# Two of seven low parts of weights moved from VectorE to GpSimd in a two-layer hybrid attention block

## The chip, the cores and the metric

The kernel runs on one core of a Trainium2 chip. The metric is the device time of one execution in microseconds: the median of the runs of a kernel, all made on the same chip. Engines are called by their roles: TensorE (PE, and PEld for its weight loads), VectorE (DVE), ScalarE (ACT), GpSimd (POOL) and SyncE (SP, which issues DMAs).

## What is computed

Two layers of a block that mixes sparse attention with multi-scale pooling, on 528 tokens (16 meta tokens and 512 of x) of width 1024, in float32:

```python
def hybrid_layer(x, norm_g, w_in, ..., w_a, w_b, w_out, cos, sin, k_top):
    h = rms_norm(x, norm_g)
    proj = jnp.einsum('btd,de->bte', h, w_in)
    q, k, v, gate_a, u_b, gate_b, q_idx, k_idx, w_idx, merge = jnp.split(proj, ..., axis=-1)
    ...
    attn = indexer_sparse_attention(q, k, v, q_idx, k_idx, w_idx, k_top).reshape(B, T, D_A)
    y_a = jnp.einsum('bte,ed->btd', attn * jax.nn.silu(gate_a), w_a)
    pooled = multiscale_pool(u_b, pool_w, pool_b, pool_s)
    y_b = jnp.einsum('bte,ed->btd', pooled * jax.nn.silu(gate_b), w_b)
    g_a, g_b = jnp.split(jax.nn.sigmoid(merge), 2, axis=-1)
    return x + jnp.einsum('btd,de->bte', g_a * y_a + g_b * y_b, w_out)
```

The attention of each block of 128 queries keeps the 128 best keys by an index score (top-k) and takes a softmax over them.

## The kernel before

Activations are kept with the width on the partitions and the tokens along the free axis. Each float32 operand of a large product is split into a high part (a cast to a shorter format, made on ScalarE) and a low part (the operand less its high part), and a product is three matmuls: high by high, low activation by high weight, high activation by low weight. PSUM banks are called d (products), a (scores, transposes) and v (attention values).

The projections for gate_a and merge, and half of w_out in the second layer, use a scheme of seven products for a two by two matrix of blocks, in place of eight. `mixed_prep` (line 257) prepares one chunk of weights for that: it names the seven weight operands a11, a12, s2, s1, s3, s4, a22 by the blocks that they are made from. For each, `hi` (line 265) casts the high part on ScalarE and `lo` (line 271) subtracts it for the low part, a 128x512 tile called w in the profile. Three DMAs and subtractions make the sums among them: `first_sum` (line 253) adds the block a11 to a21 by an accumulating DMA of GpSimd's queue (L255 in the profile), line 284 adds s2 to a12 by another one (L284), and VectorE makes s2 (tile s) and s1 (into tile raw). The steps are the items `i0` to `i8`, which are put into a queue. `group_of_products` (line 1044) issues the seven products in the order a11, a12, s2, s1, s3, s4, a22, each of 12 matmuls: for each of four rows of blocks high by high, high by low, and only with the third matmul the low part of the weights. Between the products it takes items from the queue, so that a weight operand is prepared some products ahead. What a product leaves in PSUM goes to ScalarE (`out`, copies p and u) or to VectorE (`total`, the additions c, or sila in a layer's first two groups), and frees the bank.

There are ten such groups in each layer (`mix_gates`, line 1099) and two at the end (`mix_out`, line 1198), 22 in all. In order of time they are numbered 0 to 9 (about 167 to 305 us), 10 to 19 (525 to 660) and 20 and 21 (704 to 726). Beside them runs the attention, a generator from which some steps are taken between products: logits on TensorE; their sum with the selection's mask on VectorE (lt, with the minimum mn, which a 128x2 product then scales); the exponential and the scaling by rs on ScalarE; the first 16 columns, scaled, in pm on GpSimd (L847); and their split px (cast on ScalarE, subtraction on GpSimd, L881).

The order of TensorE's and VectorE's instructions is the written one; that of ScalarE's and GpSimd's is set by the framework's scheduler when the kernel is built. Each engine works in order. The top-k selection on VectorE (MAX and MATCH_REPLACE on tiles sc) has no place of its own. `Metered` wrappers add up an estimated cost of every instruction that is written to TensorE and to VectorE, and after each product `group_done` takes steps of the selection as long as VectorE's estimate lags:

```python
spare[0] += share[0] * (pe.us - seen[0]) - (dve.us - seen[1])
...
while spare[0] > 0 and sel:
```

Of the kernel before, what the change touches and what calls it, by code (L numbers as in the profile page):

```python
# [91 lines left out]
def tile_block(ctx: ExitStack, tc: tile.TileContext, x, meta, w_in, pool_w, w_a, w_b, w_out, rows, hgain, c_tab, out):  # L92
    nc = tc.nc
    act, gp = nc.scalar, nc.gpsimd
    pe, dve = Metered(nc.tensor, pe_cost), Metered(nc.vector, dve_cost)
# [7 lines left out]
    def f(ap):  # L103
        return ap.bitcast(F32)
# [53 lines left out]
    def w_load():  # L158
        if W["load"] < len(chunks):
            c = w_place()  # L160
            for s in range(2):
                w_fetch(c, s)
# [10 lines left out]
    def w_tile():  # L173
        return wpool.tile([128, 1024], F32R, tag="w", name="w", bufs=8)
# [74 lines left out]
    def marked():  # L249

        return tc.issue_after(mark[0]) if mark[0] else nullcontext()

    def first_sum(c):
        if c in mixed:
            gp.dma_start(raws[c][0][:, 1], raws[c][0][:, 0], accum_op=OP.add)  # L255

    def mixed_prep(c):

        r0, r1 = raws[c]
        blk = {"a11": r0[:, 0], "a21": r0[:, 1], "a12": r1[:, 0], "a22": r1[:, 1]}  # L260
        src = {"a11": "a11", "a12": "a12", "a22": "a22", "s3": "a21", "s2": "s2", "s1": "a11", "s4": "a12"}
        ops = ready[c]
        soon = c <= len(chunks) - 2

        def hi(n):
            t = w_tile().rearrange("p (s k e) -> p s k e", s=2, k=4)
            ops[n] = t
            with marked():
                act.copy(t[:, 0], blk[src[n]])  # L269

        def lo(n):
            dve.tensor_sub(ops[n][:, 1], blk[src[n]], f(ops[n][:, 0]))

        def i0():
            hi("a12")
            if soon:
                hi("a11")

        def i1():
            lo("a12")  # L280
            blk["s2"] = tmp.tile([128, 544], F32, tag="L", name="s2", bufs=LB)[:, :512].rearrange(
                "p (k e) -> p k e", k=4)
            dve.tensor_add(blk["s2"], blk["a21"], blk["a22"])
            gp.dma_start(blk["a12"], blk["s2"], accum_op=OP.add)  # L284
            (lo if soon else hi)("a11")

        def i2():
            if not soon:
                lo("a11")
            dve.tensor_sub(blk["a11"], blk["s2"], blk["a11"])  # L290

        def i3():
            hi("s2")

        def i4():
            lo("s2")
            hi("s1")

        def i5():
            lo("s1")  # L300
            hi("s3")

        def i6():
            lo("s3")
            hi("s4")
            first_sum(c + 1)

        def i7():
            lo("s4")
            hi("a22")  # L310

        def i8():
            lo("a22")
            del raws[c]
            w_load()

        def counted(fn):
            def item():
                fn()
                progress[c] += 1  # L320
            return item

        progress[c] = 0
        return [counted(fn) for fn in (i0, i1, i2, i3, i4, i5, i6, i7, i8)]
# [1311 lines left out]
```

## Time and profile before

| | us |
|---|---|
| median of 3 runs | 734.77 (734.75 to 734.92) |
| the profiled execution | 735.03 |
| its span, first to last instruction | 733.2 |
| TensorE busy | 723.7 |
| VectorE busy | 597.2 |
| ScalarE busy | 491.4 |
| GpSimd busy | 262.3 |

TensorE's clock was granted in full over the whole span. A busy time is the union of an engine's instructions. Matmuls overlap, and the ends of their spans are modelled, so that a stall is better read from a matmul's start and the start of the one before it, or from the idle time of the weight loads. Each line of an instruction gives its start, its time, the engine, the line, the operation, the tiles written and read, the shape, the count, and in square brackets the idle time before it with what ended it.

### The profile page before, as it was taken

Reading aid. Unit: us, or ns where it says so; the run is one execution under the profiler, and the core shown is the slowest. Engines: PE = TensorE matmul, PEld = TensorE weight load, DVE = VectorE, ACT = ScalarE, POOL = GpSimd, SP = SyncE. Lnnn points to the kernel's source line nnn. Section 1 sums busy time; section 2 is a strip of 40 time slices with the busy share of each in tenths; the row PEclk is TensorE's granted clock in tenths of the full one; section 3 lists DMA queues with packets and bytes.
Section 4 is the critical chain, followed back from the end, with each engine's and each line's share of the span. In section 5 each row is a group of like instructions: output and inputs, shape, how many; then the busy total and the mean of one; then the engine's idle time right before and its main releaser. Section 6 shows DMA issues by size and latency. Waiting matters only on the chain.

```text
span 733.2 us, 15958 instructions
## 1 busy us (share of the span) xinstructions
PE 723.7 (99%) x5853; PEld 697.0 (95%) x5853; DVE 597.2 (81%) x1488; ACT 491.4 (67%) x1125; POOL 262.3 (36%) x345
## 2 busy tenths in 40 slices
PE   9999999999999999999999999999999999999998
PEld 8999998899999999999999989998899899999997
DVE  6877999998998875894358779999989988768774
ACT  6779635676888886543246796367788888775643
POOL 3751174721223311173256411857042231116210
PEclk9999999999999999999999999999999999999999
DMA  8777755974655333633422788667564554438832
GB/s 268 234 180 166 168 138 116 238 149 91 148 113 136 81 92 97 211 124 130 132 89 87 180 185 200 155 162 163 112 160 105 134 116 91 113 108 269 201 90 71
DMA packets 103566, 106.41 MB, mean 145 GB/s; under 512 B 5008, under 2 KB 83632, under 8 KB 103488
## 3 DMA queue, kind: packets, MB, share of 16 engines
q1 hardware_dynamic: 91888, 74.89, 33.5%
q0 software_dynamic: 11520, 30.41, 23.4%
q8 instruction: 46, 0.75, 0.4%
q14 instruction: 32, 0.26, 0.1%
q10 hardware_dynamic: 80, 0.08, 0.0%
HBM read 66.41 MB, written 8.55 MB: 102 GB/s over the span
## 4 chain that ended last, share of the span: by engine, by line
PE 79%; DVE 12%; issue 4%; ACT 2%; DMA 2%; POOL 1%; DVEq 0%; POOLq 0%; ACTq 0%
PE d L63 65%; PE a L63 10%; PE v L63 4%; DVE w L63 3%; DVE t L63 1%; DVE lt L63 1%; DMA w<-raw 1%; DVE sc L63 1%; DVE m L63 1%; ACT lt L832 1%; DVE zb L63 1%; DVE nf L63 1%; DVE c L63 0%; DMA raw<-s 0%; DVE sila L63 0%
## 5 line engine op out<-in xcount | busy, mean ns | idle before, releaser
L63 PE MATMUL d<-hhi,w 128*128 128x256 f32 (+3 forms) x1392 | 279.2, 292 | 1.6 <-DVE c L63 1.6
L63 PEld LDWEIGHTS d<-hhi,w 128*128 128x128 f32 x1392 | 222.3, 188 | 5.2 <-DVE c L63 2.0
L63 PE MATMUL d<-hlo,w 128*128 128x256 f32 (+3 forms) x696 | 189.8, 289 | 0.0
L63 DVE TENSOR_TENSOR w<-raw,w 128x512 fp32r<-128x512 f32 (+1 forms) x156 | 121.8, 787 | 14.5 <-ACT w L269 14.3
L63 PEld LDWEIGHTS d<-hlo,w 128*128 128x128 f32 x696 | 131.3, 189 | 1.4 <-issue 0.2
L63 PE MATMUL d<-hsum,w 128*128 128x264 f32 (+1 forms) x720 | 95.1, 285 | 0.2
L63 PEld LDWEIGHTS d<-hsum,w 128*128 128x128 f32 x720 | 89.7, 188 | 1.2 <-issue 0.3
L63 PE MATMUL d<-w,hhi 128*128 128x256 f32 x576 | 86.1, 287 | 0.6 <-DVE w L63 0.6
L269 ACT CAST w<-raw 128x512 fp32r<-128x512 f32 x132 | 78.5, 623 | 3.0 <-DMA raw<-s 2.3
L63 PEld LDWEIGHTS d<-w,hhi 128*128 128x128 f32 x576 | 74.7, 188 | 5.3 <-issue 2.9
L255 POOL DMA_DIRECT2D raw<-raw x22 | 20.5, 931 | 109.3 <-DMA raw<-in_w_in_dram 16.3
L63 DVE MATCH_REPLACE8 sc<-m,sc 128x400 f32<-128x400 f32 (+2 forms) x100 | 54.4, 547 | 0.0
L63 DVE MAX8 m<-sc 128x8 f32<-128x400 f32 (+2 forms) x100 | 53.4, 557 | 0.9
L221 POOL DMA_DIRECT2D w<-raw x34 | 31.8, 966 | 60.9 <-ACT w L220 44.7
L832 ACT ACTIVATE lt<-lt,mn,NR 128x144 f32<-128x144 f32 (+3 forms) x64 | 42.2, 661 | 13.2 <-DVE mn L63 13.0
L63 PE MATMUL d<-mhi,w 128*128 128x272 f32 (+2 forms) x192 | 46.1, 326 | 1.0 <-ACT sq L681 0.9
L63 PE MATMUL d<-w,hlo 128*128 128x256 f32 x288 | 45.5, 281 | 0.0
L284 POOL DMA_DIRECT2D raw<-s x22 | 19.2, 871 | 65.5 <-DVE s L63 29.0
L847 POOL TENSOR_SCALAR pm<-lt,rs 128x16 f32<-128x16 f32 x48 | 28.0, 612 | 38.8 <-DVE rs L63 28.6
L753 ACT ACTIVATE r<-a,wab 128x272 f32<-128x272 f32 (+2 forms) x80 | 35.5, 487 | 8.7 <-PE a L63 8.2
L1481 POOL TENSOR_TENSOR hlo<-ta,hhi 128x256 fp32r<-128x256 f32 (+1 forms) x28 | 26.6, 961 | 40.9 <-PE d L63 28.7
L690 POOL TENSOR_TENSOR t<-t,t 128x256 f32<-128x256 f32 (+1 forms) x34 | 30.6, 900 | 24.6 <-DVE t L63 24.3
(259 smaller groups left out, 1566.2 us busy)
## 6 DMA issues: line engine op xcount, KB each, us to landing
raw<-in_w_in_dram SPq DMA_DIRECT2D x88, 256.0 KB, 3.3
w<-raw POOLq DMA_DIRECT2D x34, 512.0 KB, 5.8
raw<-in_w_in_dram SPq DMA_DIRECT2D x32, 512.0 KB, 4.3
raw<-in_w_out_dram SPq DMA_DIRECT2D x12, 512.0 KB, 3.6
raw<-raw POOLq DMA_DIRECT2D x22, 256.0 KB, 4.0
raw<-s POOLq DMA_DIRECT2D x22, 256.0 KB, 3.3
kept<-res SPq DMA_DIRECT2D x16, 264.0 KB, 2.8
res<-kept SPq DMA_DIRECT2D x16, 264.0 KB, 5.2
```

The lines of the kernel that those rows point to most:

```text
L63: return fn(*a, **k)
L221: gp.dma_start(t, raws[c][s], accum_op=OP.add)
L255: gp.dma_start(raws[c][0][:, 1], raws[c][0][:, 0], accum_op=OP.add)
L269: act.copy(t[:, 0], blk[src[n]])
L284: gp.dma_start(blk["a12"], blk["s2"], accum_op=OP.add)
L690: added[0] = gp.tensor_tensor(t1[:m, :256], t1[:m, :256], t2[:m, :256], op=OP.add).ins
L753: act.activation(r[:, n - 1::-1] if i == 0 else r[:, o:o + e], ps[:, :e], AF.Relu, scale=wab[:, i, h:h + 1])
L832: act.activation(L[hh][:, :n], L[hh][:, :n], AF.Exp, scale=NR[:, i, h:h + 1], bias=mn[:, hh:hh + 1], accum_out=sm[:, hh:hh + 1])
L847: (gp if j < 3 else dve).tensor_scalar(pms[i][:, 2 * j + hh, :], L[hh][:, 0:16], rs[:, hh:hh + 1], None, op0=OP.mult)
L1481: pool_end = gp.tensor_sub(hlo[:, j, a:a + n], d, f(hhi[:, j, a:a + n]))
```

## The change

In `lo`, the low parts of the operands s3 and s4 are subtracted by GpSimd (`gp`) and not by VectorE (`dve`); the other five stay. `gp` is not metered, so the selection's rule no longer counts them. The high parts, the DMAs and the products are as before.

```diff
         def lo(n):
-            dve.tensor_sub(ops[n][:, 1], blk[src[n]], f(ops[n][:, 0]))
+            (gp if n in ("s3", "s4") else dve).tensor_sub(ops[n][:, 1], blk[src[n]], f(ops[n][:, 0]))
```

TensorE's instructions stand in the same order as before, row for row. On GpSimd's queue, at the first groups of the first layer, from group 0's sum s2 on (s_2452), the new subtractions (L272) stand between the accumulating DMAs and the pm scalings. Before:

```order
L255 DMA raw<-raw 128x512
L284 DMA raw<-s_2452 128x512
L255 DMA raw<-raw 128x512
L284 DMA raw<-s_2658 128x512
L847 TENSOR_SCALAR pm<-lt,rs 128x16 x4
L255 DMA raw<-raw 128x512
L284 DMA raw<-s_2846 128x512
```

And now:

```order
L284 DMA raw<-s_2452 128x512
L272 TENSOR_TENSOR w<-raw,w 128x512 x2
L255 DMA raw<-raw 128x512
L284 DMA raw<-s_2659 128x512
L847 TENSOR_SCALAR pm<-lt,rs 128x16 x2
L272 TENSOR_TENSOR w<-raw,w 128x512 x2
L847 TENSOR_SCALAR pm<-lt,rs 128x16 x2
L255 DMA raw<-raw 128x512
```

Two subtractions a group went in, behind the group's s2 DMA and in front of the next group's first sum.

On VectorE, at the same groups, a low part (w<-raw,w) goes out and a step of the selection comes in early; the steps are MATCH_REPLACE on sc_993, which before stood 23 rows further on:

```order
 L63 TENSOR_TENSOR mn<-mn,RQ 128x2
-L63 TENSOR_TENSOR w<-raw,w 128x512 x2
+L63 TENSOR_TENSOR w<-raw,w 128x512
+L63 MATCH_REPLACE sc_993<-m_2528,sc_993 128x528
 L63 TENSOR_TENSOR sila<-d,p_2628 128x264
 L63 SCALAR_TENSOR_TENSOR sila<-th,sila 128x264
```

One low part of group 0 left, and the selection's step moved up from group 1.

On VectorE in group 14, in the second layer (s_8176 before, s_8180 now, is that group's s2), where the selection ended before and the steps of the attention for the third block of queries begin (sc_6126):

```order
 L63 SCALAR_TENSOR_TENSOR zb<-th,zb 128x256
-L63 TENSOR_TENSOR w<-raw,w 128x512 x2
-L63 MATCH_REPLACE sc_6126<-m_8094,sc_6126 128x400
-L63 MATCH_REPLACE sc_6178<-m_8116,sc_6178 128x528
-L63 TENSOR_SCALAR sc_6126<-sc_6126 128x400
-L63 TENSOR_SCALAR sc_6178<-sc_6178 128x528
-L63 TENSOR_TENSOR c<-d,p_8254 128x256
+L63 TENSOR_TENSOR w<-raw,w 128x512
+L63 TENSOR_TENSOR c<-d,p_8258 128x256
 L63 RECIPROCAL rs<-sm 128x2
 L63 TENSOR_SCALAR pm<-lt,rs 128x16 x2
-L63 TENSOR_TENSOR w<-raw,w 128x512
```

Both low parts and the end of the selection left this place; the selection now ends in group 13.

## Rows read from the trace of the kernel before

**Rows 1.** The page's head: span, and busy time (share) and instructions by engine

```profile
span 733.2 us, 15958 instructions
PE 723.7 (99%) x5853; PEld 697.0 (95%) x5853; DVE 597.2 (81%) x1488; ACT 491.4 (67%) x1125; POOL 262.3 (36%) x345
```

**Rows 2.** Busy time by stretch: length, PE, PEld, DVE, ACT, POOL, clock, DMA, GB/s

```profile
186.60:223.00 36.40, 36.29 (x304) 35.66 (x304) 36.23 (x97) 29.95 (x76) 10.01 (x14) 1.00 0.59 130
223.00:303.00 80.00, 79.56 (x715) 76.97 (x713) 60.14 (x164) 64.45 (x150) 17.57 (x26) 1.00 0.42 103
...
543.50:587.00 43.50, 41.88 (x352) 40.97 (x351) 43.22 (x117) 37.06 (x96) 13.76 (x18) 1.00 0.56 125
```

**Rows 3.** Timeline of the weight loads: start, time, what, idle time before

```profile
218.54 0.54 PEld L63 LDWEIGHTS d<-hsum,w 128*128 128x128 f32 x4 [0.32 <-DVE w L63]
...
584.81 0.19 PEld L63 LDWEIGHTS d<-hhi,w 128*128 128x128 f32 x1 [1.78 <-DVE c L63]
...
707.29 0.89 PEld L63 LDWEIGHTS d<-osum,w 128*128 128x128 f32 x7 [0.34 <-DVE w L63]
```

**Rows 4.** Timeline of TensorE: the last matmul ahead of that of 584.81

```profile
582.96 0.28 PE L63 MATMUL d<-hhi,w 128*128 128x256 f32 x1
```

**Rows 5.** Timeline in group 14, VectorE and GpSimd

```profile
577.75 0.56 DVE L63 MATCH_REPLACE8 sc<-m,sc 128x400 f32<-128x400 f32 x1
...
579.52 0.42 DVE L63 TENSOR_TENSOR c<-d,p 128x256 f32<-128x256 f32 x1
...
582.37 1.45 DVE L63 TENSOR_TENSOR mn<-mn,RQ 128x2 f32<-128x2 f32 x1
...
582.77 1.02 POOL L881 TENSOR_TENSOR px<-pm,px 128x256 fp32r<-128x256 f32 x1
...
584.35 0.41 DVE L63 TENSOR_TENSOR c<-d,p 128x256 f32<-128x256 f32 x1
```

**Rows 6.** VectorE's groups by shape: count, busy us, mean ns, idle before

```profile
L63 DVE TENSOR_TENSOR w<-raw,w 128x512 fp32r<-128x512 f32 x132 | 90.1, 687 | 14.5 <-ACT w L269 14.3
...
L63 DVE TENSOR_TENSOR ta<-ta,zb 128x256 f32<-128x256 f32 x24 | 14.3, 598 | 0.8
...
L63 DVE TENSOR_TENSOR osum<-ta,osum 128x256 fp32r<-128x256 f32 x16 | 6.0, 420 | 0.6 <-ACT osum L1150 0.5
```

**Rows 7.** Timeline of VectorE and GpSimd around the px of 645 us

```profile
645.58 1.81 POOL L881 TENSOR_TENSOR px<-pm,px 128x256 fp32r<-128x256 f32 x1 [11.18 <-ACT px L880]
...
646.12 0.69 DVE L63 TENSOR_TENSOR w<-raw,w 128x512 fp32r<-128x512 f32 x1
...
646.72 0.42 DVE L63 TENSOR_TENSOR c<-d,u 128x256 f32<-128x256 f32 x1
```

**Rows 8.** Timeline of GpSimd: instructions with two inputs

```profile
113.22 1.09 POOL L1398 TENSOR_TENSOR us<-u 128x543 f32<-128x543 f32 x1 [0.17 <-ACT u L1391]
...
663.17 0.73 POOL L1481 TENSOR_TENSOR hlo<-ta,hhi 128x256 fp32r<-128x256 f32 x1 [14.94 <-PE d L63]
```

**Rows 9.** Timeline in group 13: casts of s3 and s4, product s3

```profile
564.38 1.14 ACT L269 CAST w<-raw 128x512 fp32r<-128x512 f32 x2
...
567.50 1.58 PE L63 MATMUL d<-hsum,w 128*128 128x256 f32 x12
```

**Rows 10.** Timeline of VectorE and GpSimd around the px of 202 us

```profile
202.42 0.74 POOL L881 TENSOR_TENSOR px<-pm,px 128x256 fp32r<-128x256 f32 x1 [0.67 <-ACT px L880]
...
202.47 1.24 DVE L63 TENSOR_TENSOR raw<-s,raw 128x512 f32<-128x512 f32 x1
```

**Rows 11.** Timeline, group 3's start: first low part, third matmul

```profile
200.26 0.69 DVE L63 TENSOR_TENSOR w<-raw,w 128x512 fp32r<-128x512 f32 x1
...
201.33 0.41 PE L63 MATMUL d<-hhi,w 128*128 128x264 f32 x2
```

**Rows 12.** Timeline of VectorE in group 20: the last low part

```profile
711.10 0.69 DVE L63 TENSOR_TENSOR w<-raw,w 128x512 fp32r<-128x512 f32 x1
```

**Rows 13.** Timeline of TensorE, group 20: third matmul of s4

```profile
711.90 0.28 PE L63 MATMUL d<-hhi,w 128*128 128x256 f32 x1
```

## The prediction

> **What bounds the kernel now.** I read the page's head first, then busy time by stretch, then what TensorE's weight loads waited for, then the rows of VectorE and GpSimd at those places. TensorE is busy for 723.7 of 733.2 us, VectorE for 597.2, GpSimd for 262.3 [rows 1]. A change that leaves TensorE's instructions and their order as they are, as this one does, can win only what TensorE now waits, so the reader should look for those waits and not at VectorE's share. The changed work lies in the 22 groups of seven products, 0 to 21 in order of time. Two stretches matter: from 186.6 to 223 us (groups 2 to 4) VectorE is busy 36.23 of 36.40 us, and from 543.5 to 587 us (groups 12 to 14) 43.22 of 43.50; behind the first it has room, 60.14 of 80.00 [rows 2]. In both stretches the top-k selection (MAX and MATCH_REPLACE) runs on VectorE between the low parts. In the groups the weight loads wait for VectorE in a way worth naming at three places: 0.32, 1.78 and 0.34 us [rows 3]. The 1.78 is the prize. Its matmul starts at 584.81, 1.85 us behind the last one at 582.96 [rows 3, 4], where matmuls of this size otherwise follow each other by (1.58 - 0.28)/11 = 0.12 [rows 9]; so 1.73 us are lost. The chain behind it on VectorE: the end of the top-k (577.75 to 579.52), the 128x2 product mn that took 1.45 us, and at 584.35 the addition c that empties the PSUM bank which the next product wants [rows 5]. Beside that long mn GpSimd ran px [rows 5].
>
> **What leaves VectorE.** 44 low parts, two for each of 22 groups. One takes 0.69 us in the mean [rows 6], and what comes behind it starts 0.60 us later (646.12, 646.72) [rows 7]. So 44 x 0.60 = 26.4 us of VectorE's time. Almost none of it is TensorE's: outside the two stretches it falls on idle time.
>
> **What the order does with it.** The two low parts are not metered any more, so the rule that spends VectorE's spare time pulls top-k steps forward. I count in the new order, with 0.60 us for a low part and 0.6 for a top-k step (577.75 to 579.52 holds two replacements and two short closing steps [rows 5]). Up to the s2 sum of group 3 six low parts are gone (3.6 us) and six steps, some 3.5 us, have come forward: VectorE has gained 0.1 us. Up to group 4's it has gained 2.5, since the top-k now ends in group 3 instead of 4, and up to group 5's 6.0. In the second layer it is the same: nothing gained up to group 13, 2.5 us up to group 14, and the top-k is over before the chain of rows 5 begins.
>
> **What GpSimd takes on.** No row has this subtraction on GpSimd. The nearest: two inputs of 256 columns alone, 0.73 us, and of 543 columns, 1.09 [rows 8]. On the line between them 512 columns cost 0.73 + 256 x 0.36/287 = 1.05 us, the lower end. The upper end is the px at 645.58, which took 1.81 us beside VectorE subtractions that also read two SBUF tensors [rows 7]. I take 1.05, since most of the time VectorE is at something else, and keep 1.81. 44 x 1.05 = 46 us fit into GpSimd's 471 idle us. Is it in time? The tightest s3 is group 13's: two casts start at 564.38 and take 1.14 together, so the first is done at about 565.0; the product begins at 567.50 and wants the low part with its third matmul, 0.24 later [rows 9]. That leaves 2.7 us for 1.05 to 1.81, so 0.9 at the least for what stands in front on GpSimd's queue (pm, an accumulating DMA). s4 comes a product later. I cost the wait for GpSimd itself at nothing here; without that cover it would be up to 1 us a group.
>
> The Trainium skill, page "GPSIMD Engine Reference", section "4.1 Engine selection", speaks against the change: elementwise work on a tile belongs on VectorE, since GpSimd is about 2 times slower with two inputs. By that the subtraction would take 2 x 0.69 = 1.4 us, an estimate from that page, and only step 4 of the sum below would grow, by 0.35; the lengths of rows 8 are shorter than that.
>
> **What the two engines cost each other.** At 202.42 GpSimd's px starts, and VectorE's raw subtraction, 0.05 later, takes 1.24 us [rows 10] instead of about 0.69 [rows 6]: it gets through when px is done. At 645.58 it is the other way: px sits through the subtraction of 646.12 and is done 0.67 us after VectorE turned, at 646.72, to the addition c, which reads PSUM [rows 7]. So only instructions with two SBUF inputs wait. The price of one moved subtraction to VectorE lies between 0 (VectorE is in the top-k or reads PSUM) and 1.05 (all of it). The additions ta<-ta,zb, beside which GpSimd subtracts 256 columns, give a middle: 598 ns against 420 for the same size in osum [rows 6], 0.18 more, or 0.26 at 1.05/0.73 the length. I take 0.4 where two meet, between that and the 0.55 of rows 10, and not every one meets: behind s1's low part, when GpSimd starts, the new order mostly has top-k steps.
>
> **The sum.** (1) The wait at 584.81: two low parts of group 14 (1.2 us) and the end of the top-k (577.75 to 579.52, 1.8 us) leave its chain, 3.0 us against 1.73: gone, -1.73. (2) The 0.32 of group 4 goes with its top-k: -0.3. (3) Group 3's first low part is done at 200.95 and wanted at 201.33 [rows 11], 0.38 us to spare; VectorE has gained nothing there and meets group 2's two subtractions, 2 x 0.4: 0.8 - 0.4 = +0.4, and as much by halves in the second layer: +0.3. (4) Group 20: its last low part on VectorE, at 711.10, would start 0.6 earlier, at 710.5; the work before it reads two SBUF tensors without a gap, so s4's subtraction gets through at about 711.1; 711.1 + 1.05 = 712.15 [rows 12], and the third matmul wants it at 711.90 [rows 13]: +0.25. Together -1.73 - 0.3 + 0.4 + 0.3 + 0.25 = -1.1 us. The profiled execution, 735.03 us, would come to 733.9, the median, 734.77, to 733.7. The 1.8 us around the span stay.
>
> **The rivals.** A, everything covered: no meeting costs anything, and 1.73 + 0.32 + 0.34 = 2.4 us go: 732.4. For it: the top-k reads one tensor. Against: the long mn and raw. B, the port, slower: in each full stretch four subtractions (groups 2 and 3, 12 and 13) fall where the order gives VectorE nothing, and each holds it for 0.7 us, two thirds of 1.05. That is 2.8 us late in each, less 0.38 to spare as in rows 11: 2 x 2.4 - 2.0 = +2.8, 737.6. It decides from 0.35 us per subtraction on (8 x 0.35 - 0.76 = 2.0, what steps 1 and 2 win). For it: rows 5 and 10. Against: rows 7, where VectorE kept its pace. The Trainium skill, page "SBUF — State Buffer", section "🔬 SBUF: two separate sides", has it that whoever starts first keeps the shared port pair for the whole instruction and the other fully blocks, which is this rival taken to the letter; rows 10 agree. C, the wait only moves: the chain of rows 5 gets shorter, but the bank is emptied late for another reason (ScalarE's copies, or px), and nothing is left: 734.8. That GpSimd isn't used is excluded by its new order.
>
> **How the numbers follow.** Forecast 42%, centre 733.7, by its terms 732.9 to 734.7; A 15%; B 28%, 735.7 to 738; C 15%. A measurement of this kernel tells about 0.2% (1.5 us) from no change, so faster is under 733.3, slower over 736.2. A third of the forecast and all of A are faster: 0.30. B but for a fifth is slower: 0.22. The rest, 0.48, is within. The range from 732.0 to 737.6 leaves out A's lowest part and B's upper half.
>
> **What the next profile would show.** Step 1: no wait near 583 us, and MATCH_REPLACE over before group 14. Step 3: a weight load that waits for VectorE's w near 201. Step 4: one that waits for GpSimd near 712. For the price: the 128x512 subtraction on GpSimd at 1.05 to 1.5 us in the mean. If mn, raw and zb on VectorE are longer by over 0.35 us per moved subtraction, B is right. If weight loads wait for GpSimd's w in many groups, my 2.7 us were wrong.

## The result

The changed kernel takes 738.96 us (median of 6 runs, 737.95 to 739.31) against 734.76 (734.41 to 735.58) for the kernel before on the same chip: 1.0051 times as long, 95% interval 1.0040 to 1.0061. In a second comparison it was 1.0039 (1.0025 to 1.0053). The forecast was a gain of 1.1 us; the kernel lost 4.2.

The page's head of the changed kernel, which answers [rows 1]:

```profile
span 736.2 us, 16046 instructions
PE 724.2 (98%) x5853; PEld 696.8 (95%) x5853; DVE 585.1 (79%) x1444; ACT 492.1 (67%) x1125; POOL 319.5 (43%) x389
```

TensorE's work is the same (723.7 before). VectorE lost 44 instructions but only 12.1 of the 26.4 us forecast, and GpSimd gained 57.2 us, not 46. The busy time of the stretches of [rows 2], in that view's columns, says that TensorE now idles where it was full:

```profile
186.60:223.00 36.40, 35.83 (x300) 35.07 (x299) 33.48 (x85) 29.72 (x77) 18.07 (x21) 1.00 0.58 129
223.00:303.00 80.00, 78.75 (x708) 76.16 (x708) 55.29 (x151) 64.00 (x151) 30.53 (x35) 1.00 0.43 100
543.50:587.00 43.50, 41.05 (x342) 39.68 (x342) 40.21 (x103) 36.30 (x96) 19.54 (x23) 1.00 0.55 122
```

TensorE issues the same matmuls in the same order, so the two traces can be laid over each other: the start of a group's first matmul less its start before, and how that grows over a group. Over groups 0 to 21 it grows by 3.11 us, and in the second profile of the same kernel by 3.08, no place differing by more than 0.05. Ahead of group 0, where the change has done nothing yet, those two executions differ by 1.09 us (first matmul at 167.02 and 168.11): so much moves from one execution to the next. The two intervals, 2.9 to 4.5 us and 1.8 to 3.9 us, both hold the 3.1 us, and those are taken for the change here. By place, with the experiments told below beside it ("counted" is e1_metered, "order" e2_order_only, "pm away" e4_pm_away, "halves" e6_halves, "both" e9_halves_counted):

| us | changed | counted | order | pm away | halves | both |
|---|---|---|---|---|---|---|
| group 1 | +0.61 | 0.00 | +0.49 | +0.57 | +0.47 | 0.00 |
| group 2 | +1.13 | +0.64 | +1.77 | +1.49 | +0.13 | 0.00 |
| group 4 | -0.57 | -0.01 | -0.57 | -0.57 | -0.57 | +0.11 |
| group 7 | +0.81 | +0.82 | +0.01 | +0.81 | +0.01 | -0.02 |
| groups 8 to 10 | -0.64 | -0.67 | +0.02 | -0.67 | -0.63 | -0.63 |
| group 12 | +2.15 | +1.10 | +1.55 | 0.00 | +1.29 | +0.01 |
| group 13 | +0.60 | -0.14 | -0.12 | -0.12 | +0.04 | -0.12 |
| group 14, up to a22 | +0.49 | +0.74 | -0.16 | +0.29 | +0.50 | +0.72 |
| group 14, a22 | -1.74 | -1.74 | -1.74 | -1.74 | -1.74 | -1.74 |
| groups 20, 21 | +0.29 | +0.26 | -0.05 | +0.30 | +0.26 | +0.27 |
| all 22 groups | +3.11 | +1.12 | +1.21 | +1.11 | -0.04 | -1.05 |

(The places left out change by at most 0.12, but for three: "pm away" loses 0.65 behind group 14, "halves" 0.19 in group 11, and "both" 0.47 in group 3.) A group is counted to the start of the next one, so that the row "groups 8 to 10" holds the time between groups 9 and 10 as well. The two waits that the prediction meant to win were won, -1.74 and -0.57. What TensorE's weight loads wait for now (start, time, what, in brackets the idle time and what ended it), in groups 1, 2, 7, 12, 12 and 13:

```profile
181.86 0.66 PEld L63 LDWEIGHTS d<-hsum,w 128*128 128x128 f32 x5 [0.46 <-ACT p L1071]
197.90 0.67 PEld L63 LDWEIGHTS d<-hsum,w 128*128 128x128 f32 x5 [0.79 <-ACT u L1071]
273.17 0.78 PEld L63 LDWEIGHTS d<-hsum,w 128*128 128x128 f32 x6 [1.12 <-ACT u L1071]
558.41 0.19 PEld L63 LDWEIGHTS d<-hhi,w 128*128 128x128 f32 x1 [1.51 <-ACT p L1071]
561.28 0.19 PEld L63 LDWEIGHTS d<-hhi,w 128*128 128x128 f32 x1 [0.51 <-DVE c L63]
570.19 0.42 PEld L63 LDWEIGHTS d<-hsum,w 128*128 128x128 f32 x3 [0.55 <-DVE w L63]
```

None waits for GpSimd's w. Mostly it is ScalarE's copy out of PSUM (p, u) that comes late, and VectorE is behind that. The longest, in group 12, from the timelines of GpSimd, VectorE and ScalarE (the row of 1.19 us is the first of the two pm by itself, that of 2.43 both):

```profile
552.75 2.54 POOL L272 TENSOR_TENSOR w<-raw,w 128x512 fp32r<-128x512 f32 x2 [2.45 <-ACT w L269]
...
552.89 1.19 DVE L63 TENSOR_SCALAR pm<-lt,rs 128x16 f32<-128x16 f32 x1
...
552.89 2.43 DVE L63 TENSOR_SCALAR pm<-lt,rs 128x16 f32<-128x16 f32 x2
...
556.95 0.40 DVE L63 TENSOR_TENSOR c<-d,p 128x256 f32<-128x256 f32 x1
...
557.38 0.42 ACT L1117 ACTIVATE c<-c 128x256 f32<-128x256 f32 x1 [2.40 <-DVE c L63]
...
558.00 0.36 ACT L1071 COPY p<-d 128x256 f32<-128x256 f32 x1
```

GpSimd subtracts twice, 552.75 to 555.29. VectorE's two scalings pm, 128 by 16 elements and 0.23 us each elsewhere, take 2.43 together; the first is done at 554.08, 0.04 behind GpSimd's first subtraction (552.75 and 1.29), the second at 555.32, 0.03 behind its second. They sit out one subtraction each. Behind them three selection steps stand ahead of c (556.95), and ScalarE, which works in order, waits 2.40 us for c with the copy p behind it. For p waits the product of 558.41. A blocked instruction shows as a long one here, not as idle time: the reader must compare it with others of its form.

### The profile page after: what moved, and what is told of

The parts are those of the page before. It is cut to its first block, busy times and chain, and to the rows that moved or that the text cites. A ratio compares the mean times of both kernels' runs of the same rounds, so it can differ in the third digit from the quotient of the medians.

```text
span 736.2 us, 16046 instructions
## 1 busy us (share of the span) xinstructions
PE 724.2 (98%) x5853; PEld 696.8 (95%) x5853; DVE 585.1 (79%) x1444; ACT 492.1 (67%) x1125; POOL 319.5 (43%) x389
## 4 chain that ended last, share of the span: by engine, by line
PE 81%; DVE 10%; ACT 4%; issue 3%; POOL 1%; DVEq 0%; POOLq 0%; ACTq 0%
PE d L63 67%; PE a L63 10%; PE v L63 4%; DVE w L63 3%; DVE lt L63 1%; ACT lt L832 1%; DVE t L63 1%; DVE sila L63 1%; ACT w L269 1%; DVE s L63 1%; DVE nf L63 1%; DVE c L63 0%; POOL w L272 0%; DVE hlo L63 0%; DVE sc L63 0%
## 5 line engine op out<-in xcount | busy, mean ns | idle before, releaser
L63 DVE TENSOR_TENSOR w<-raw,w 128x512 fp32r<-128x512 f32 (+1 forms) x112 | 96.6, 866 | 15.0 <-ACT w L269 14.9
L272 POOL TENSOR_TENSOR w<-raw,w 128x512 fp32r<-128x512 f32 x44 | 60.7, 1395 | 52.6 <-ACT w L269 52.4
```

What stands on the lines that cost most here:

```text
L63: return fn(*a, **k)
L272: (gp if n in ("s3", "s4") else dve).tensor_sub(ops[n][:, 1], blk[src[n]], f(ops[n][:, 0]))
```

## The experiments

Two theories for the 3.1 us. **The port**: instructions of VectorE wait while GpSimd subtracts, as in the prediction's rival B. **The order**: the steps of the selection that come forward make VectorE late for work that stands behind them. A third, that the products wait for GpSimd's low parts, the rows above exclude: the tightest of the 44 is done at 542.80 and wanted at 544.14, 1.34 us to spare.

### The subtractions moved, the selection left in place

```diff
             (gp if n in ("s3", "s4") else dve).tensor_sub(ops[n][:, 1], blk[src[n]], f(ops[n][:, 0]))
+            dve.us += 0.6025 * (n in ("s3", "s4"))
```

> The moved subtractions are credited to VectorE's estimate as if it still made them, so the selection's steps stand where they stood before; only the 44 subtractions themselves change engine. Theory 1 (the port: VectorE's instructions whose tensors all lie in SBUF wait until GpSimd's subtraction is done) keeps the losses that the trace after shows beside GpSimd, 2.7 to 4.2 us (group 2: 1.0, group 7: 0.8, group 12: up to 1.5, group 13: 0.6, groups 20 and 21: 0.3), and wins back about 1.5 us in groups 4 and 14, where VectorE has two subtractions less: 735.9 to 737.5. Theory 2 (the order: selection steps pulled ahead make VectorE late) has no loss left: 733.0 to 733.5.

Measured 736.95 us, 1.0025 (1.0016 to 1.0034), about half of what the change cost. The table has the port's loss in groups 2, 7 and 12, without the 0.6 of group 1. The 0.74 of group 14 is mostly another matter ("A third cause", below).

### The order alone

```diff
-            dve.tensor_sub(ops[n][:, 1], blk[src[n]], f(ops[n][:, 0]))
+            (dve.engine if n in ("s3", "s4") else dve).tensor_sub(ops[n][:, 1], blk[src[n]], f(ops[n][:, 0]))
```

> All seven low parts stay on VectorE, but two of them are no longer counted, so the selection's steps come forward as in the changed kernel. Theory 1 (the port): no long instruction of VectorE beside GpSimd; the order alone costs what it cost in groups 1 and 14 of the trace after (0.4 and 0.6) and wins the waits of groups 4 and 14 in part, since VectorE has all its subtractions: 733.8 to 735.5. Theory 2 (the order): the loss is here in full, 738 to 739.

Measured 736.71 us, 1.0018 (1.0010 to 1.0026): between the two, so neither theory alone holds. GpSimd makes none of the low parts here, and still group 1 loses 0.49 us. This run overstates the order: the steps come forward as in the changed kernel, but VectorE still makes all 44 low parts, so that it has more to do up to each place. The 1.77 of group 2 is more than the changed kernel lost there. The rows that show how, VectorE in group 1 of the changed kernel:

```profile
175.15 0.69 DVE L63 MATCH_REPLACE8 sc<-m,sc 128x528 f32<-128x528 f32 x1
175.76 0.42 DVE L63 TENSOR_TENSOR sila<-d,p 128x264 f32<-128x264 f32 x1
```

The step that came forward stands just ahead of an addition that empties a bank, and everything behind is 0.6 us later, up to mn, the exponentials that need it, and p behind them on ScalarE. In group 2 of the kernel with the order alone another step stands ahead of the c of 201.15, for which TensorE waits:

```profile
200.68 0.56 DVE L63 MATCH_REPLACE8 sc<-m,sc 128x400 f32<-128x400 f32 x1
201.15 0.42 DVE L63 TENSOR_TENSOR c<-d,p 128x264 f32<-128x264 f32 x1
...
201.63 0.39 PE L63 MATMUL d<-hhi,w 128*128 128x264 f32 x1 [0.97 <-DVE c L63]
```

And the order alone wins the 1.74 at group 14's a22, as the move alone does: either is enough. The two losses, 0.25% and 0.18%, come to 0.43% against the 0.51 and 0.39 measured for the change, and both runs hold the same win of 1.74. By place they don't add up (group 2: 0.64 and 1.77, together 1.13), since a late VectorE can be late for both reasons at once, and since this run keeps the 44 low parts on VectorE.

### The waiting scalings taken off VectorE

```diff
-                (gp if j < 3 else dve).tensor_scalar(pms[i][:, 2 * j + hh, :], L[hh][:, 0:16], rs[:, hh:hh + 1], None, op0=OP.mult)
+                gp.tensor_scalar(pms[i][:, 2 * j + hh, :], L[hh][:, 0:16], rs[:, hh:hh + 1], None, op0=OP.mult) if j < 3 else act.activation(pms[i][:, 2 * j + hh, :], L[hh][:, 0:16], AF.Copy, scale=rs[:, hh:hh + 1])
```

> The changed kernel, with the 16 small scalings pm (128x16) that VectorE makes handed to ScalarE. In the trace after, two pairs of them sat through both subtractions of GpSimd, 2.4 us in group 12 and 2.6 us in group 14. Theory 1 (the port): the 1.46 us that TensorE lost before group 12's s4 go for the most part, 739.0 - 1.0 to 1.5 = 737.5 to 738.0, and c in group 12 comes some 2 us earlier. Theory 2 (the order): c there is late because of the selection's steps ahead of it, so 738.5 to 739.5.

Measured 736.63 us, 1.0019 (1.0011 to 1.0027). The 2.15 us of group 12 and the 0.60 of group 13 are gone ("pm away" in the table), and c in group 12 comes 1.82 us earlier, with the same selection steps ahead of it:

```profile
555.13 0.40 DVE L63 TENSOR_TENSOR c<-d,p 128x256 f32<-128x256 f32 x1
```

Against the changed kernel it loses 0.36 in group 2 and 0.76 behind group 14 (0.65 against -0.11); ScalarE has 16 more instructions in this run; in group 2 a selection step moved up as well, so there the two can't be told apart. So the two pm, 32 columns in all, and what ran late behind them carried some 2.9 us, more than expected.

### The changed kernel again, and GpSimd's subtraction cut in two

The changed kernel was run once more beside the halves of this section and two versions that follow below (one subtraction a group, and group 14's pair alone):

> The changed kernel once more, beside the three others on one chip, so that they can be set against it and not only against the kernel before. 1.004 to 1.006 of the kernel before by either theory.

It took 738.43 us, 1.0039 (1.0025 to 1.0053). In halves:

```diff
-            (gp if n in ("s3", "s4") else dve).tensor_sub(ops[n][:, 1], blk[src[n]], f(ops[n][:, 0]))
+            for k in ((slice(0, 2), slice(2, 4)) if n in ("s3", "s4") else (slice(0, 4),)):
+                (gp if n in ("s3", "s4") else dve).tensor_sub(ops[n][:, 1, k], blk[src[n]][:, k], f(ops[n][:, 0, k]))
```

> The changed kernel, with each of the 44 subtractions of GpSimd made as two of 256 columns, about 0.7 us each in place of 1.29. Theory 1a (the port is held for one instruction, and a waiting VectorE comes next): the longest delay of an instruction of VectorE falls from 1.1 to about 0.65 us, the two pm of group 12 lose 1.2 in place of 2.1, and the kernel wins 0.8 to 1.5 us on the changed one. Theory 1b (GpSimd's next instruction takes the port ahead of a waiting VectorE): the delays grow to the length of both halves, 1.3 us or more, and the time is that of the changed kernel or up to 1 us more. Theory 2 (the order): no difference within 0.3 us.

Measured 735.63 us, 1.0007 (0.9998 to 1.0017): 2.8 us less than the changed kernel on the same chip, more than the 0.8 to 1.5 expected, though GpSimd works longer. VectorE's and ScalarE's instructions stand in the same order in the two traces, row for row, so neither the selection's order nor ScalarE's can have made the difference. The forms of GpSimd's low part and of pm on VectorE (shortest, median and longest, ns), first in the changed kernel, then in halves:

```profile
L272 POOL TENSOR_TENSOR w<-raw,w x44: 1272/1292/1822, 170.2 to 722.4; 128x512 fp32r<-128x512 f32 x44
L63 DVE TENSOR_SCALAR pm<-lt,rs x16: 226/230/1358, 199.0 to 647.4; 128x16 f32<-128x16 f32 x16
```

```profile
L273 POOL TENSOR_TENSOR w<-raw,w x88: 717/735/1259, 171.0 to 721.1; 128x256 fp32r<-128x256 f32 x88
L63 DVE TENSOR_SCALAR pm<-lt,rs x16: 222/232/805, 198.6 to 645.1; 128x16 f32<-128x16 f32 x16
```

The longest pm went from 1.13 to 0.58 us above the usual 0.23, which is the first of the two variants: VectorE got its turn between two halves. In group 12 the pair takes 1.32 us, not 2.43:

```profile
552.13 2.83 POOL L273 TENSOR_TENSOR w<-raw,w 128x256 fp32r<-128x256 f32 x4 [2.75 <-ACT w L269]
...
552.27 1.32 DVE L63 TENSOR_SCALAR pm<-lt,rs 128x16 f32<-128x16 f32 x2
```

The loss of group 7 is gone, that of group 2 but for 0.13, and the order's in group 1 stays, as the two theories share them out.

### In quarters

```diff
-            dve.tensor_sub(ops[n][:, 1], blk[src[n]], f(ops[n][:, 0]))
+            there = n in ("s3", "s4")
+            for k in ((slice(0, 1), slice(1, 2), slice(2, 3), slice(3, 4)) if there else (slice(0, 4),)): (gp if there else dve).tensor_sub(ops[n][:, 1, k], blk[src[n]][:, k], f(ops[n][:, 0, k]))
```

> The changed kernel (not credited), each subtraction of GpSimd in four of 128 columns, about 0.42 us each. If the price is one instruction of GpSimd that is under way, VectorE's longest delay falls to about 0.35 us and the kernel comes to 735 or less; if a waiting VectorE must stand back at each new instruction, the delays add up to those of halves again, 735.5 to 737.

Measured 735.66 us, 1.0003 (0.9994 to 1.0012): no better than halves. GpSimd's part of a low part:

```profile
L273 POOL TENSOR_TENSOR w<-raw,w x176: 445/461/985, 170.9 to 722.0; 128x128 fp32r<-128x128 f32 x176
```

Four times 0.461 are 1.84 us for what took 1.29. VectorE's delays did get shorter: over all rows that ran 0.05 us or more above the median of their form, they come to 16.8 us in the changed kernel, 11.3 in halves and 8.3 in quarters, none over 0.34 but one. New waits in group 11 (+1.12) take what that gives, and the one long delay, 0.76, stands at their head:

```profile
539.93 1.79 POOL L273 TENSOR_TENSOR w<-raw,w 128x128 fp32r<-128x128 f32 x4
...
540.82 0.92 DVE L63 TENSOR_TENSOR mn<-mn,RQ 128x2 f32<-128x2 f32 x1
```

This mn started while GpSimd was at the second of four quarters and ended 0.03 behind the fourth, which was done at 541.72. So VectorE does not get its turn between every two instructions of GpSimd; what decides it is not shown.

### One subtraction a group

```diff
-            (gp if n in ("s3", "s4") else dve).tensor_sub(ops[n][:, 1], blk[src[n]], f(ops[n][:, 0]))
+            (gp if n == "s3" else dve).tensor_sub(ops[n][:, 1], blk[src[n]], f(ops[n][:, 0]))
```

> One subtraction a group is moved, that for s3, and not counted; so GpSimd never makes two in a row, and half as many selection steps come forward. Theory 1 (the port): no delay of VectorE is longer than one subtraction, the two pm of group 12 lose at most 1.1 together, and the port's part of the loss is half or less: 1.002 to 1.0035 of the kernel before. Theory 2 (the order): half the steps, half the loss, 1.0025.

Measured 735.56 us, 1.0000 (0.9991 to 1.0008), under both expectations. Half the change keeps all of the two gains (-0.57 and -1.74) and has about half of the losses: 3.3 us against 6.2, summed over the groups and parts of groups that lose. The losses go with what is moved, the gains do not.

### The subtractions as extra work

```diff
             dve.tensor_sub(ops[n][:, 1], blk[src[n]], f(ops[n][:, 0]))
+            n in ("s3", "s4") and gp.tensor_sub(blk["a11"], blk[src[n]], f(ops[n][:, 0]))
```

> The kernel before with everything in place, and GpSimd makes the 44 subtractions a second time, into a block that is dead by then; nothing reads what it writes. VectorE's order is word for word that of before. Theory 1 (the port): 734.8 plus 2.7 to 4.2 us, and no relief: 737.5 to 739; pm, mn and the low part of s1 on VectorE take up to 1.1 us longer beside GpSimd. Theory 2 (the order): nothing moves, 734.8.

Measured 747.14 us, 1.0161 (1.0145 to 1.0177), far more than the port was to cost, and not a clean measure of it. The block written must be free first, so the subtractions and the accumulating DMAs behind them on GpSimd's queue come later; ScalarE's cast of s4 then waits for that DMA. Its waits from 167 to 310 us (total, times, longest):

```profile
ACT w L269 <- DMA raw<-s: 8.4, 5, 3.4
```

In the kernel before that was 1.1. VectorE's and ScalarE's orders are those of before, and beside these subtractions 24 rows of VectorE are over 0.3 us longer than elsewhere, 19 us together: the delays need no new order. What they cost here can't be told from what the late DMAs cost.

### Versions that keep the gain

Only group 14's pair, and credited (counted for VectorE as in the first experiment):

```diff
-            (gp if n in ("s3", "s4") else dve).tensor_sub(ops[n][:, 1], blk[src[n]], f(ops[n][:, 0]))
+            there = n in ("s3", "s4") and sum(m < c for m in mixed) in (14,)
+            (gp if there else dve).tensor_sub(ops[n][:, 1], blk[src[n]], f(ops[n][:, 0])); dve.us += 0.6025 * there
```

> Only the two subtractions of group 14 are moved, and credited as before, so that everything up to group 14 is word for word the kernel before. Theory 1 (the port): the moved pair stands at the chain of the 1.73 us wait alone; VectorE saves 1.2 us there, but its pair pm, its mn or its subtraction for a22 meets GpSimd's pair and loses 1 to 2 us of it again: between 733.4 (the wait goes, as in the changed kernel) and 734.8 (nothing). Theory 2 (the order): 733.0, the wait goes and nothing is lost.

Measured 734.30 us, 0.9989 (0.9981 to 0.9998). The wait is won (-1.74) and 0.60 lost again: s1's low part, started 0.3 us behind GpSimd's subtraction, takes 1.78 us, and TensorE then waits for the scaled exponentials lt behind it:

```profile
576.56 1.55 POOL L273 TENSOR_TENSOR w<-raw,w 128x512 fp32r<-128x512 f32 x1 [0.97 <-ACT w L269]
...
576.87 1.78 DVE L63 TENSOR_TENSOR w<-raw,w 128x512 fp32r<-128x512 f32 x1
```

The weight loads' waits from 570 to 590 us there (total, times, longest):

```profile
PEld a L63 <- ACT lt L846: 0.6, 2, 0.3
```

All 44 in halves, credited:

```diff
-            (gp if n in ("s3", "s4") else dve).tensor_sub(ops[n][:, 1], blk[src[n]], f(ops[n][:, 0]))
+            there = n in ("s3", "s4"); dve.us += 0.6025 * there
+            for k in ((slice(0, 2), slice(2, 4)) if there else (slice(0, 4),)): (gp if there else dve).tensor_sub(ops[n][:, 1, k], blk[src[n]][:, k], f(ops[n][:, 0, k]))
```

> Both causes taken away as far as that goes: each subtraction of GpSimd in two halves, and credited to VectorE's estimate, so that the selection stands where it stood before. If port and order together are the loss, what is left is about 1.3 us of small delays against 2.0 us won in groups 4 and 14: 734.0 to 735.0, no different from the kernel before, with no loss in groups 1, 2 and 7. If a third cause is in it (the low parts come too late, or ScalarE's order), 735.5 or more.

Measured 734.44 us, 0.9987 (0.9978 to 0.9996). Groups 1, 2, 7 and 12 cost nothing any more: with both taken away, nothing of the loss is left there. Against "counted" only the halving differs, and VectorE's and ScalarE's instructions stand in the same order, so the step from +1.12 to -1.05 us over all groups is the port by itself. Two further kernels took a part of the groups for it. Groups 4 and 14 alone:

```diff
-            there = n in ("s3", "s4"); dve.us += 0.6025 * there
+            there = n in ("s3", "s4") and sum(m < c for m in mixed) in (4, 14); dve.us += 0.6025 * there
```

> Only groups 4 and 14, in halves, credited: the places at which TensorE waited for VectorE before. By the port and the order together: -1.7 in group 14 and -0.3 in group 4, and 0.3 to 0.6 lost again beside GpSimd: 733.2 to 733.8, ratio 0.998 to 0.999, the fastest of these kernels.

Measured 734.82 us, 0.9995 (0.9987 to 1.0004), over the 733.2 to 733.8 expected: group 4's halves cost 1.05 us and win nothing. All but groups 3 and 4:

```diff
-            there = n in ("s3", "s4"); dve.us += 0.6025 * there
+            there = n in ("s3", "s4") and sum(m < c for m in mixed) not in (3, 4); dve.us += 0.6025 * there
```

> The halved and credited version without groups 3 and 4, in whose stretch it lost 0.5 and 0.6 us and won 0.4 (0.3 and 0.1). If those losses come from GpSimd's halves there (the port), 0.6 to 1.0 us less than the halved and credited version: 733.5 to 733.9, ratio 0.9975 to 0.9985. If they come from ScalarE's order, which the scheduler sets anew for the whole kernel, no gain: 0.9987.

Measured 734.76 us, 0.9993 (0.9983 to 1.0003). Its trace has 0.00 in group 3 and -0.34 in group 4, where "both" has +0.47 and +0.11 (-1.89 over all groups against -1.05), but the timed runs, on another chip, don't bear that out: the intervals overlap. The fastest versions gain about 0.1%, below the 0.2% that the prediction held for telling, though two intervals exclude no change.

## Why the prediction was wrong

**Where the gain was, held.** Step 1 (the wait of [rows 3, 5] goes, -1.73) came out at -1.74, step 2 (-0.3) at -0.57 with the matmuls around it. But the reason for step 1 was named too broadly: the order alone wins that wait, and so does the move alone. Step 2 is the order's, as the prediction said.

**GpSimd's own time was taken too low.** It is 1.29 us where nothing is in the way (median of 44), not 1.05: the line through two instructions of other kinds [rows 8] misled, and the mean is 1.395. This alone cost nothing: with 1.34 us or more to spare the wait for GpSimd's low parts stayed at nothing, as costed. Step 4 (+0.25 for s4 in group 20) was wrong in its reason. That part was done at 713.03 and wanted at 714.49; counted from the group's first matmul, it was done 6.5 us in and wanted 8.0 us in, where the prediction had it done 8.2 us in. GpSimd did not stand back behind VectorE's work: VectorE's osum sat beside it, for 1.51 us instead of 0.42, and groups 20 and 21 lost 0.29 by that. The Trainium skill, page "GPSIMD Engine Reference", section "4.1 Engine selection", had the subtraction at about twice VectorE's time; the trace agrees, 1.29 against VectorE's 0.683.

**The step that failed is the price of a meeting.** "I take 0.4 where two meet", and ahead of it "so only instructions with two SBUF inputs wait". Of the changed kernel's VectorE rows, 19 that ran beside a moved subtraction took over 0.3 us longer than the median of their form elsewhere, 15.8 us together and 0.83 in the mean, up to 1.13. By form, the longest excess: pm 1.13 and lt 0.84 (TENSOR_SCALAR, one tensor in SBUF and a column of factors), sc 0.38 (TENSOR_SCALAR too, a closing step of the selection), mn 1.07 (128x2, 0.16 us otherwise), low parts 1.10, osum 1.09, res 0.65. mn's form (shortest, median and longest, ns):

```profile
L63 DVE TENSOR_TENSOR mn<-mn,RQ x32: 160/161/1234, 171.5 to 639.0; 128x2 f32<-128x2 f32 x32
```

Spread over the 44 moved subtractions the 15.8 us are 0.36 each, just above the 0.35 that the prediction set as the sign of rival B. Beside the same subtractions MATCH_REPLACE, MAX, the RECIPROCAL of 128x2 and everything that reads PSUM (c, sila<-d, lt<-a,sc) were longer by at most 0.01. So, for a form that waits, the delay is what is left of GpSimd's instruction, however small the one that waits. The middle of 0.26 from ta<-ta,zb [rows 6] was a mean over instructions that met late or not at all, and the delay of [rows 10], 0.55, had met an instruction of 0.74 us, little more than half of the new one. The Trainium skill, page "SBUF — State Buffer", section "🔬 SBUF: two separate sides", names besides instructions with two SBUF inputs those in a two-port performance mode as held up for the whole instruction; the pm rows agree, if pm runs in such a mode. The prediction had weighed only its half on two inputs. No row names pm's mode, but its forms tell how fast they run: in the kernel before, undisturbed, the scaling lt<-lt,rs (pm's instruction on more columns) takes 0.487 us for 512 columns and 0.421 for 384, 0.52 ns a column, where MATCH_REPLACE, which was not held up, takes 1.05. That fits a faster mode for pm's instruction, and proves none:

```profile
L63 DVE TENSOR_SCALAR lt<-lt,rs 128x512 f32<-128x512 f32 x8 | 3.9, 487 | 0.3
L63 DVE TENSOR_SCALAR lt<-lt,rs 128x384 f32<-128x384 f32 x8 | 3.4, 421 | 0.3
...
L63 DVE MATCH_REPLACE8 sc<-m,sc 128x528 f32<-128x528 f32 x32 | 22.1, 691 | 0.0
L63 DVE MATCH_REPLACE8 sc<-m,sc 128x400 f32<-128x400 f32 x32 | 17.8, 557 | 0.0
```

**The place was wrong with it.** Step 3 put +0.4 on group 3's first low part, which still made it by 0.29 us (done 202.67, wanted 202.96), and +0.3 on its like in the second layer. The cost lay where the delayed instruction has a queue behind it: s1's low part in group 2 (1.45 us) and then mn (0.68), so that the exponentials hold up u on ScalarE, +0.73; in group 7 s1's low part (1.58) and lt (1.33), where VectorE had 19.9 us to spare in the stretch [rows 2] and was late all the same, +0.81; pm in group 12. The rows of group 2:

```profile
193.04 3.40 POOL L272 TENSOR_TENSOR w<-raw,w 128x512 fp32r<-128x512 f32 x2 [1.28 <-ACT w L269]
...
193.85 1.45 DVE L63 TENSOR_TENSOR w<-raw,w 128x512 fp32r<-128x512 f32 x1
...
195.78 0.68 DVE L63 TENSOR_TENSOR mn<-mn,RQ 128x2 f32<-128x2 f32 x1
```

The sentence that behind s1's low part "the new order mostly has top-k steps" overlooked that low part itself.

**The order was summed, not placed.** "VectorE has gained 0.1 us" up to group 3 added up its work; a step that moves ahead of c or sila makes the bank late by its own 0.6 us even where the sum is even. That was costed at nothing. Between kernels whose low parts are made alike and whose selection stands in the new place or the old, it is worth 2.0 us ("changed" against "counted", 3.11 and 1.12) and 1.0 us ("halves" against "both", -0.04 and -1.05); ScalarE's order differs a little in these pairs too.

Rival B was nearest in mechanism, the port in groups 2, 3, 12 and 13 at 0.7 us for each of eight subtractions: those groups lost 3.87 us against its 4.8. But those 3.87 hold a part of the order as well, and B missed groups 1 and 7, and so its 737.6 and the range end below the 738.96.

**A third cause.** In group 14 the exponentials now stand ahead of the copy p on ScalarE (in the trace of before p ran at 575.21 and the exponentials from 575.99). The scheduler sets that order anew for each kernel:

```profile
579.59 0.60 ACT L832 ACTIVATE lt<-lt,mn,NR 128x272 f32<-128x272 f32 x1
...
580.19 0.35 ACT L1071 COPY p<-d 128x256 f32<-128x256 f32 x1
...
580.59 0.53 PEld L63 LDWEIGHTS d<-hsum,w 128*128 128x128 f32 x4 [0.63 <-ACT p L1071]
```

No run changed this order alone, but the traces sort by it. In the eight with the exponentials ahead (the changed kernel twice, "counted", "pm away", "halves", "both", the quarters, and all but groups 3 and 4) the product that waits for p begins 0.42 to 0.86 us later against the matmul before it; in the five with p ahead ("order", the extra work, one subtraction a group, group 14 alone, and groups 4 and 14 alone) the difference is 0.00. The prediction's sum had no term for that; its rival C named ScalarE's copies as a reason.

**Left open.** Some 0.6 us come back in most kernels in which GpSimd makes low parts. They lie between groups 9 and 10: two waits of TensorE in the kernel before, 0.22 us at 507.75 for ScalarE's sq and 0.50 at 516.43 for a DMA of weights, are not there in the changed kernel. Why they go was not followed.

## What to carry to other kernels

Work given to GpSimd is paid for by VectorE where VectorE's next instruction reads two tensors from SBUF, or is a TENSOR_SCALAR from SBUF to SBUF as pm and lt are (MATCH_REPLACE, MAX and RECIPROCAL, which read SBUF too, paid nothing): cost each meeting at up to the whole of GpSimd's instruction (0.83 us in the mean of 1.29 here), look at which small instruction stands there and what waits for it, and try GpSimd's work in pieces (halves won 2.8 of 3.2 us here, quarters no more). Spare time in a stretch is no cover for that. Where a rule or meter places other work by counted time, moving an instruction out of the count moves that work too: undo the two apart (move and count; don't move and don't count) before blaming either. And where a scheduler sets an engine's order, compare that order before and after as well.

## What was not expected of the hardware

- An instruction of VectorE of 128x2 elements took 1.23 us beside a GpSimd subtraction, one of 128x16 1.36, ending some 0.03 us behind GpSimd each time; with GpSimd's instructions back to back, two pm in a row each sat one out, while one mn of 128x2 sat through more than two of GpSimd's quarters (0.92 us).
- GpSimd's subtraction with 128, 256 and 512 columns took 0.461, 0.735 and 1.292 us (medians): about 0.18 us and 2.2 ns a column. VectorE's took 0.683 for 512.
- It goes the other way as well: GpSimd's subtraction took up to 1.82 us where VectorE's instructions with two SBUF inputs were already running.
